# Feed-forward layers of a hybrid encoder by seven block products of sums instead of eight plain ones

## The chip, the cores and the metric

The kernel runs on one core of one Trainium2 chip. The metric is the device time of one execution in microseconds (us); less is better. The engines are TensorE (PE, with its weight loads as PEld), VectorE (DVE), ScalarE (ACT), GpSimd (POOL) and SyncE (SP), which issues nearly all DMA. Each engine works through its own queue in order and waits on semaphores.

## The reference, cut to what matters

1536 tokens of 1024 features (a sequence of 1024 and one of 512) pass one encoder layer in float32. The middle part (a long convolution and a retention mixer) is not touched by the change.

```python
def swiglu(h, w1, w3, w2):
    return (jax.nn.silu(h @ w1) * (h @ w3)) @ w2      # w1, w3 [1024, 2816], w2 [2816, 1024]
...
    h = rmsnorm(x, p['ffn1_pre_g'])
    x = x + 0.5 * rmsnorm(swiglu(h, p['ffn1_w1'], p['ffn1_w3'], p['ffn1_w2']), p['ffn1_post_g'])
    h = rmsnorm(x, p['mix_pre_g'])
    ...                                               # w_in, the two mixers, w_out
    x = x + rmsnorm(y, p['mix_post_g'])
    h = rmsnorm(x, p['ffn2_pre_g'])
    x = x + 0.5 * rmsnorm(swiglu(h, p['ffn2_w1'], p['ffn2_w3'], p['ffn2_w2']), p['ffn2_post_g'])
```

## The kernel before, in words

Activations lie as features (128 partitions, eight blocks) by tokens. Every float32 operand of a matmul is split into a float32r head (`hi_act`, a copy on ACT) and the rest (`lo`, a subtraction on DVE or POOL), and every product is three matmuls (`mm3`, lines 66 to 68): head by head, head by rest, rest by head.

A feed-forward layer (`ffn_phase`) takes the tokens in three groups of 512. `ffn_up` loops over 22 blocks of 128 hidden features; each block loads 1 MB of weights (w1 and w3 together), splits them, and makes 2 times 8 times 3 matmuls of 512 columns into two banks of PSUM. The factor of the first rmsnorm is applied behind the matmuls (L205, L207), so the matmuls do not wait for it. `proj` then makes 22 times 8 times 3 matmuls with w2, and `post` normalizes, adds the residual and stores, 512 tokens at a time. In source order the next group's `norm_T` stands ahead of `proj`, and the last part of `post` runs while the next group's up matmuls run. The splits of weights go to DVE and POOL in turn. The first layer's last group is followed by the norm for `w_in`; the second layer's first norm stands behind the last `out_proj`, with its pools opened early.

A tile scheduler with a timeline of its own sets the order in which each engine's instructions stand, within what data and buffers allow; a pool's `bufs` is the number of buffers that its tiles share.

Of the kernel before, what the change touches and what calls it, by code (L numbers as in the profile page):

```python
# [15 lines left out]
D = 1024  # L16
# [30 lines left out]
class Kern:  # L47
# [16 lines left out]
    def mm3(self, ps, ah, al, bh, bl, first, last):  # L64
        mm = self.nc.tensor.matmul
        mm(ps, lhsT=ah, rhs=bh, start=first, stop=False)  # L66
        mm(ps, lhsT=ah, rhs=bl, start=False, stop=False)  # L67
        mm(ps, lhsT=al, rhs=bh, start=False, stop=last)  # L68
# [16 lines left out]
    def rstd(self, ssq, scale, half=False, eng=None):  # L85
        """(ssq * scale + eps) ** -0.5, times a half when asked"""
# [15 lines left out]
    def rstd_rows(self, acc, psp, rp, tag, half=False, **kw):  # L102
        """acc [128, 512]: sums of squares left to add over the partitions -> DRAM row: the factor of
        rmsnorm of each of the 512 columns; and the tile that can take it"""
# [8 lines left out]
        out = rp.tile([128, 512], F32, tag=tag, name="rrow", **(kw or {"bufs": 1}))  # L113
# [3 lines left out]
        r = self.rstd(c, 1.0 / D, half)  # L117
        row = self.dp.tile([1, 512], F32, name=f"row{self.rows}")
        self.rows += 1
        nc.sync.dma_start(row.rearrange("o (p c) -> (o p) c", c=4), r)  # L120
        return row, out
# [12 lines left out]

    def add_sq(self, acc, x, out, first):
# [9 lines left out]
    def norm_T(self, src, gi, psp, hp, late, row, eng=None, between=None, xp=None):  # L145
# [7 lines left out]
        if row is not None:  # L153
            r = self.np.tile([128, 512], F32, tag="rpre", name="rrow", bufs=1)
            nc.sync.dma_start(r, row.broadcast_to([128, 512]))
        else:
            acc = self.np.tile([128, 512], F32, tag="acc", name="acc", bufs=1)
        for i in range(4):
            x = self.xp.tile([128, 2, 512], F32, tag="x", name="x") if xp is None else \
                xp.tile([128, 2, 512], F32, tag=f"z{2 * i}", name="x", bufs=1)  # L160
            nc.sync.dma_start(x, src[i])
            if i == 1 and between:
                between()
            for j in range(2):
                k = 2 * i + j
                g = self.gains[:, gi, k:k + 1]
                if late:
                    nc.scalar.activation(hh[:, k], x[:, j], AF.Copy, scale=g)  # L168
                    nc.vector.scalar_tensor_tensor(hl[:, k], x[:, j], g, hh[:, k].bitcast(F32), ALU.mult, ALU.subtract)  # L169
                else:  # L170
                    nc.vector.scalar_tensor_tensor(x[:, j], x[:, j], g, r, ALU.mult, ALU.mult)
                    self.hi_act(hh[:, k], x[:, j])
                    self.lo(eng or nc.vector, hl[:, k], x[:, j], hh[:, k])
            if row is None:
                self.add_sq(acc, x, x, i == 0)
        if row is None:
            row, r = self.rstd_rows(acc, psp, self.np, "rpre")
            nc.sync.dma_start(r, row.broadcast_to([128, 512]))
        return (hh, hl, r) if late else (hh, hl)

    def ffn_up(self, hT, w13, up, psp, wp, rp, first=None):
        nc = self.nc
        hh, hl, r = hT
        th, tl = [], []
        for f in range(NF):
            u = up[f * len(up) // NF]
            th.append(u.tile([128, 512], F32R, tag=f"th{f}", name="th"))
            tl.append(u.tile([128, 512], F32R, tag=f"tl{f}", name="tl"))
            raw = None if f else first
            if raw is None:  # L190
                raw = rp.tile([128, 2, KD, 128], F32, tag="raw", name="raw")
                nc.sync.dma_start(raw, w13[f])
            pab = []
            for i in range(2):
                wh = wp.tile([128, KD, 128], F32R, tag="w", name="wh")
                wl = wp.tile([128, KD, 128], F32R, tag="w", name="wl")
                self.hi_act(wh, raw[:, i])
                self.lo(nc.vector if i or first is raw else nc.gpsimd, wl, raw[:, i], wh)
                ps = psp.tile([128, 512], F32, tag="mm", name="up")
                for k in range(KD):  # L200
                    self.mm3(ps, wh[:, k], wl[:, k], hh[:, k], hl[:, k], k == 0, k == KD - 1)
                pab.append(ps)
            hid = self.tp.tile([128, 512], F32, tag="hid", name="hid", bufs=2)
            b = self.tp.tile([128, 512], F32, tag="b", name="b", bufs=1)
            nc.vector.tensor_tensor(hid, pab[0], r, ALU.mult)  # L205
            nc.scalar.activation(hid, hid, AF.Silu)
            nc.vector.tensor_tensor(b, pab[1], r, ALU.mult)  # L207
            nc.gpsimd.tensor_tensor(hid, hid, b, ALU.mult)  # L208
            self.hi_act(th[f], hid)
            self.lo(nc.vector, tl[f], hid, th[f])  # L210
        return th, tl
# [23 lines left out]
    def post(self, src, dst, gi, half, zp, psp, rows=None, op=None, cols=False):  # L235
# [6 lines left out]
        whole = op and op.tile([128, KD, 512], F32R, tag="hh", name="o").bitcast(F32)  # L242

        def done(m, ps):
# [9 lines left out]
            if op and m < 4:  # L254
                nc.sync.dma_start(whole[:, 2 * m:2 * m + 2], src[m])
            if m < KD - 1:
                return
            if cols:
                r = self.rstd_cols(acc, psp, half)
            else:  # L260
                row, r = self.rstd_rows(acc, psp, zp, "rpost", half)
                nc.sync.dma_start(r, row.broadcast_to([128, 512]))
            if rows is not None:
                a2 = zp.tile([128, 512], F32, tag="acc2", name="acc2", bufs=1)
            for i in range(4):
                if op:
                    o = whole[:, 2 * i:2 * i + 2]
                else:
                    o = self.xp.tile([128, 2, 512], F32, tag="x", name="o")
                    nc.sync.dma_start(o, src[i])  # L270
                for j in range(2):
                    nc.vector.tensor_tensor(z[i][:, j], z[i][:, j], r, ALU.mult)  # L272
                    (nc.gpsimd if j else nc.vector).tensor_tensor(z[i][:, j], z[i][:, j], o[:, j], ALU.add)  # L273
                    if op:
                        nc.sync.dma_start(dst[i][:, j], z[i][:, j])
                if not op:
                    nc.sync.dma_start(dst[i], z[i])
                if rows is not None:
                    self.add_sq(a2, z[i], o, i == 0)
            if rows is not None:  # L280
                rows.append(self.rstd_rows(a2, psp, self.xp, "x", bufs=2)[0])
        return done
# [706 lines left out]
```

## Time and profile before

| | |
|---|---|
| median of 3 runs | 3430.8 us (3430.15 to 3433.55) |
| span of the profiled execution | 3430.4 us |
| PE busy, matmuls | 3268.4 us, 95%, 15094 |
| DVE, POOL, ACT busy | 1925.7, 1290.4, 1175.4 us |
| DMA | 422.89 MB, mean 123 GB/s |

The profiled execution has no time of its own beside its span; the span is 0.4 us under the median. Matmuls are pipelined: one of 512 columns is shown as 390 ns long, but the next starts about 226 ns after it. So PE's work is to be counted by starts, not by durations. The layers of the change take 0 to 1102 us and about 2290 to 3411 us of the span.

### The profile page before, as it was taken

To read this page: it belongs to the slowest core of one execution; us is meant where nothing else is said; L and a number is where in the kernel's file an instruction comes from. 1 tells how busy PE (TensorE), PEld (TensorE's weight loads), DVE (VectorE), ACT (ScalarE), POOL (GpSimd) and SP (SyncE) were. 2 spreads that over 40 slices of the span, in tenths; PEclk is the share of its full clock that TensorE was granted. 3 is DMA by queue.
4 is the path that set the end of the run, shared out by engine and by line. 5 is a ranking of instruction groups with operands and counts; after the bars stand their busy time and mean duration, and the time that the engine had idled before them with its cause. 6 is when DMAs were issued, how large, how long until landed. Compare 5 with 4: busy or idle time off the path is not lost. (4 is left out here: it accounts for less than half of the span.)

```text
span 3430.4 us, 39206 instructions
## 1 busy us (share of the span) xinstructions
PE 3268.4 (95%) x15094; PEld 2710.5 (79%) x15094; DVE 1925.7 (56%) x2408; ACT 1175.4 (34%) x1603; POOL 1290.4 (38%) x788
## 2 busy tenths in 40 slices
PE   9999999999999899988989997989999999999998
PEld 7888788887887677766778887868888888888886
DVE  5443544435442599888877879886442444334432
ACT  4333333323332234344544344343232232323221
POOL 3332333234322422368743535554332333233322
PEclk9999999999999999989999999999999999999999
DMA  4223332324232534444354125464223432334232
GB/s 151 98 98 114 138 111 98 114 102 147 99 117 86 196 110 154 155 161 117 97 164 165 44 93 183 129 226 159 98 98 108 149 107 98 114 102 147 94 115 74
DMA packets 123275, 422.89 MB, mean 123 GB/s; under 512 B 28496, under 2 KB 37840, under 8 KB 95696
## 3 DMA queue, kind: packets, MB, share of 16 engines
q1 hardware_dynamic: 123088, 420.38, 36.1%
q8 instruction: 119, 1.95, 0.2%
q14 instruction: 68, 0.56, 0.1%
HBM read 355.73 MB, written 64.54 MB: 123 GB/s over the span
## 5 line engine op out<-in xcount | busy, mean ns | idle before, releaser
L66 PE MATMUL up<-hh,wh 128*128 128x512 f32 x2112 | 824.3, 390 | 8.3 <-ACT hh L168 8.3
L67 PE MATMUL up<-hl,wh 128*128 128x512 f32 x2112 | 824.6, 390 | 0.1
L68 PE MATMUL up<-hh,wl 128*128 128x512 f32 x2112 | 824.4, 390 | 0.0
L59 ACT ACTIVATE wh<-raw 128x1024 fp32r<-128x1024 f32 x312 | 330.0, 1058 | 783.5 <-PE up L67 635.3
L62 POOL TENSOR_TENSOR wl<-raw,wh 128x1024 fp32r<-128x1024 f32 x167 | 411.0, 2461 | 336.6 <-ACT wh L59 302.4
L208 POOL TENSOR_TENSOR hid<-hid,b 128x512 f32<-128x512 f32 x132 | 173.7, 1316 | 856.4 <-DVE b L207 830.6
L66 PEld LDWEIGHTS up<-hh,wh 128*128 128x128 f32 x2112 | 398.4, 189 | 91.3 <-ACT hh L168 8.3
L67 PEld LDWEIGHTS up<-hl,wh 128*128 128x128 f32 x2112 | 398.0, 188 | 83.4 <-DVE hl L169 0.6
L68 PEld LDWEIGHTS up<-hh,wl 128*128 128x128 f32 x2112 | 398.1, 188 | 83.0 <-DVE wl L62 0.4
L62 POOL TENSOR_TENSOR w2l<-raw,w2h 128x1024 fp32r<-128x1024 f32 x98 | 240.6, 2456 | 490.9 <-ACT w2h L59 490.9
L68 PE MATMUL proj<-th,w2l 128*128 128x512 f32 x1056 | 410.8, 389 | 0.0
L66 PE MATMUL proj<-th,w2h 128*128 128x512 f32 x1056 | 410.8, 389 | 0.0
L67 PE MATMUL proj<-tl,w2h 128*128 128x512 f32 x1056 | 410.8, 389 | 0.0
L62 DVE TENSOR_TENSOR tl<-hid,th 128x512 fp32r<-128x512 f32 x132 | 262.8, 1991 | 234.2 <-ACT th L59 233.9
L59 ACT ACTIVATE w2h<-raw 128x1024 fp32r<-128x1024 f32 x172 | 181.8, 1058 | 472.8 <-PE proj L67 364.0
L207 DVE TENSOR_TENSOR b<-up,rrow 128x512 f32<-128x512 f32 x132 | 91.1, 690 | 373.8 <-PE up L68 372.9
L62 DVE TENSOR_TENSOR w2l<-raw,w2h 128x1024 fp32r<-128x1024 f32 x74 | 101.3, 1369 | 326.6 <-ACT w2h L59 326.4
L66 PE MATMUL wips<-hh,wh 128*128 128x512 f32 x576 | 231.2, 401 | 22.0 <-DVE o L464 8.6
L66 PEld LDWEIGHTS proj<-th,w2h 128*128 128x128 f32 x1056 | 198.2, 188 | 41.2
L67 PEld LDWEIGHTS proj<-tl,w2h 128*128 128x128 f32 x1056 | 198.2, 188 | 41.2
L68 PEld LDWEIGHTS proj<-th,w2l 128*128 128x128 f32 x1056 | 198.2, 188 | 41.1
L67 PE MATMUL wips<-hl,wh 128*128 128x512 f32 x576 | 230.3, 400 | 0.0
(250 smaller groups left out, 5296.4 us busy)
## 6 DMA issues: line engine op xcount, KB each, us to landing
raw<-ffn_w SPq DMA_DIRECT2D x197, 1024.0 KB, 4.8
raw<-w_in_f SPq DMA_DIRECT2D x48, 512.0 KB, 3.7
x<-x SPq DMA_DIRECT2D x36, 512.0 KB, 4.5
o<-x SPq DMA_DIRECT2D x36, 512.0 KB, 5.0
x<-z SPq DMA_DIRECT2D x24, 512.0 KB, 4.2
raw<-w_out SPq DMA_DIRECT2D x24, 512.0 KB, 4.6
raw<-w_in_v SPq DMA_DIRECT2D x16, 512.0 KB, 3.8
tap<-fold SPq DMA_DIRECT2D x8, 1024.0 KB, 4.9
```

What stands on the lines that cost most here:

```text
L59: self.nc.scalar.activation(hi, src, AF.Copy)
L62: eng.tensor_tensor(lo, src, hi.bitcast(F32), ALU.subtract)
L66: mm(ps, lhsT=ah, rhs=bh, start=first, stop=False)
L67: mm(ps, lhsT=ah, rhs=bl, start=False, stop=False)
L68: mm(ps, lhsT=al, rhs=bh, start=False, stop=last)
L207: nc.vector.tensor_tensor(b, pab[1], r, ALU.mult)
L208: nc.gpsimd.tensor_tensor(hid, hid, b, ALU.mult)
```

## The change

Both feed-forward layers are rewritten (`ffn`). The tokens form two groups of 768, each in two halves of 384. A product of a weight matrix cut in 2 by 2 blocks with an activation matrix cut in 2 by 2 blocks, which takes eight block products, is made from seven products of sums and differences of blocks. Up (`up_unit`, 22 units for each group): rows of blocks are w1 and w3, the other cut is in the 1024 features. Seven products of 4 times 3 matmuls of 384 columns go into three banks; DVE makes four sums of weight blocks, all seven rests, and the combinations of products. Down (`down`): the cuts are in the 2816 hidden features, the 1024 outputs and the tokens. Five of the seven weight operands are sums; they are made once for each layer by `weight_sums`, which runs beside group 0's units (two steps for each unit), and kept in DRAM (`ws`). The rmsnorm is now applied to the activations ahead of the matmuls (`normed`, `operands`); group 1's normalized tokens go through DRAM (`nx`). Sums and differences of activations are made by DVE from whole quads [128, 4, 384]. In these layers POOL keeps only the power in `rstd`. x1 and x2 lie in quads, and the mixer and `out_proj` read and write 512-token groups in pieces of them (`pieces`).

```diff
+    def normed(self, src, gi, pool, row):
+        xs = []
+        for kh in range(2):
+            x = self.quad(pool, "xq")
+            nc.sync.dma_start(x, src[kh])
+            xs.append(x)
+        if row is None:
+            r = self.spread(self.rstd3(self.sum_sq(xs, pool)))
+        else:
+            r = self.half("rq")
+            nc.sync.dma_start(r, row.broadcast_to([128, 384]))
+        for kh in range(2):
+            for k in range(4):
+                g = self.gains[:, gi, 4 * kh + k:4 * kh + k + 1]
+                nc.vector.scalar_tensor_tensor(xs[kh][:, k], xs[kh][:, k], g, r, ALU.mult, ALU.mult)
+        return xs
...
+        product(ba, a11, "11", True)
+        nc.scalar.activation(p1, ba, AF.Copy)
+        tt(s[0], a21, a22, ALU.add)
+        tt(s[1], s[0], a11, ALU.subtract)
+        product(bb, s[1], "t2", True)
+        tt(u2, bb, p1, ALU.add)
+        product(ba, a12, "21", False)
+        nc.scalar.activation(hid[0], ba, AF.Silu)
+        tt(s[2], a11, a21, ALU.subtract)
+        product(bb, s[2], "t3", False)
+        tt(u3, bb, p1, ALU.add)
+        product(bc, s[0], "t1", True)
+        tt(u3, bc, u3, ALU.add)
+        product(bb, a22, "t4", False)
+        tt(p1, bb, p1, ALU.add)
+        tt(hid[0], hid[0], p1, ALU.mult)
+        tt(s[3], a12, s[1], ALU.subtract)
+        product(bc, s[3], "22", False)
+        tt(u2, bc, u2, ALU.add)
+        nc.scalar.activation(u2, u2, AF.Silu)
+        tt(hid[1], u2, u3, ALU.mult)
...
+    def weight_sums(self, w2, pool):
+        for p, ((a, *more), _) in self.FORMS.items():
+            for c in range(4) if more else ():
+                n = min(3, 11 - 3 * c)
+                ts = []
+                for q in (a, more[0]):
+                    t = self.quad(pool, "wsum").rearrange("p a b -> p (a b)")[:, :512 * n].rearrange("p (f c) -> p f c", c=512)
+                    nc.sync.dma_start(t, w2[q[0], q[1], 3 * c:3 * c + n].rearrange("f p c -> p f c"))
+                    ts.append(t)
+                nc.vector.tensor_tensor(ts[0], ts[0], ts[1], ALU.add if more[1] > 0 else ALU.subtract)
+                nc.sync.dma_start(self.ws[p][c][:, :n], ts[0])
+                yield
...
+    def post_quads(self, z, src, dst, gi, Y, row, g):
+        for th in range(2):
+            r = self.spread(self.rstd3(self.sum_sq([z[0, th], z[1, th]], Y), True))
+            for mh in range(2):
+                t = z[mh, th]
+                o = self.quad(Y, "res")
+                nc.sync.dma_start(o, src[mh][th])
+                for k in range(4):
+                    nc.vector.scalar_tensor_tensor(t[:, k], t[:, k], self.gains[:, gi, 4 * mh + k:4 * mh + k + 1], r, ALU.mult, ALU.mult)
+                for k in range(0, 4, 2):
+                    nc.vector.tensor_tensor(t[:, k:k + 2], t[:, k:k + 2], o[:, k:k + 2], ALU.add)
+                    nc.sync.dma_start(dst[mh][th][:, k:k + 2], t[:, k:k + 2])
+            if row is not None:
+                r = self.rstd3(self.sum_sq([z[0, th], z[1, th]], Y))
+                c = 768 * g + 384 * th
+                nc.sync.dma_start(row[:, c:c + 384].rearrange("o (c p) -> (o p) c", p=128), r)
...
+        with pool("xq", 6) as X, pool("yq", 20) as Y, pool("fr", 5) as self.fr, pool("fs") as self.fs, \
+                pool("fw", 10) as self.fw, pool("ft", 6) as self.ft, pool("pm", 8, space=PSUM) as self.pm:
...
+            for g in range(2):
+                for f in range(NF):
+                    self.up_unit(w13[f], [hid[fh, th][c][:, i] for th in range(2)])
+                    if f:
+                        for _ in range(2):
+                            next(side, None)
...
+                z = self.down(w2, hid, Y, at)
+                self.post_quads(z, srcs[g], dsts[g], post, Y, row_out, g)
```

How the scheduler now orders the engines is seen at three places. First PE before, in layer 1 where the first group's down products (`proj`) end and the next group's up products begin:

```order
1586 L67 MATMUL proj<-tl,w2h 128x512
1587 L68 MATMUL proj<-th,w2l 128x512
1588 L66 MATMUL up<-hh,wh 128x512
1589 L67 MATMUL up<-hl,wh 128x512
...
1622 L67 MATMUL up<-hl,wh 128x512
1623 L111 MATMUL ss<-sqs,onesr 128x512
1624 L68 MATMUL up<-hh,wl 128x512
```

The norm's sums (`ss`) stand 35 matmuls deep among the next group's up products. PE now at the end of layer 1's first group (`dn` the down products, `ss` the sums over partitions, `rps` the spread factors, `ua` the next group's first up product):

```order
2689 L69 MATMUL dn<-xh,w2l 128x384
2690 L205 MATMUL ss<-ones,acc 128x1 x3
2691 L212 MATMUL rps<-ident,r 128x128 x3
2692 L205 MATMUL ss<-ones,acc 128x1 x6
2693 L212 MATMUL rps<-ident,r 128x128 x3
2694 L205 MATMUL ss<-ones,acc 128x1 x3
2695 L67 MATMUL ua<-b11h,wh 128x384
```

All sums and spreads of both halves moved between the last down product and the first up product. DVE now at the same place (`z` the four quads of outputs, `sq` and `acc` the sums of squares, `res` the residual), from the last combination of products to the first half's last addition:

```order
653 L349 TENSOR_TENSOR z<-z,dn 128x384 x6
654 L298 TENSOR_TENSOR s_5782<-raw 128x512
655 L62 TENSOR_TENSOR wl<-s_5636,wh 128x512
656 L192 TENSOR_TENSOR sq<-sq 128x768
...
660 L195 TENSOR_TENSOR acc<-sq,acc 128x384
661 L94 TENSOR_SCALAR m<-ss 128x3
...
666 L406 SCALAR_TENSOR_TENSOR z<-z,gains,rps 128x384 x8
667 L408 TENSOR_TENSOR z<-z,res 128x768 x4
```

Behind them stand the second half's same steps and the sums for the stored factor, and only then the next group's rests of weights. The last place is SP in layer 1's first units (`raw` 256 KB of up weights, `wsum` loads of second weights, `ws` stores of their sums):

```order
6 L272 DMA raw<-ffn_w 128x512 x9
7 L329 DMA wsum<-ffn_w 128x3x512 x6
8 L329 DMA wsum<-ffn_w 128x2x512 x2
9 L272 DMA raw<-ffn_w 128x512
10 L329 DMA wsum<-ffn_w 128x3x512 x2
11 L272 DMA raw<-ffn_w 128x512
12 L332 DMA ws_1_0_179<-wsum 128x1536
13 L329 DMA wsum<-ffn_w 128x3x512
...
20 L272 DMA raw<-ffn_w 128x512 x4
21 L332 DMA ws_2_1_184<-wsum 128x1536
22 L272 DMA raw<-ffn_w 128x512 x9
```

The loads of second weights stand in bursts of eight, ahead of single loads of up weights.

## Rows read from the trace of the kernel before

**Rows 1.** The page's first part: busy us, share and instructions by engine.
```profile
PE 3268.4 (95%) x15094; PEld 2710.5 (79%) x15094; DVE 1925.7 (56%) x2408; ACT 1175.4 (34%) x1603; POOL 1290.4 (38%) x788
```
**Rows 2.** Windows: start:end, length, busy us (and instructions) by engine, granted clock, DMA share, GB/s.
```profile
0.00:100.00 100.00, 91.59 (x392) 75.33 (x393) 49.19 (x54) 41.20 (x51) 30.92 (x23) 1.00 0.44 151
200.00:420.00 220.00, 220.00 (x972) 182.15 (x971) 96.40 (x104) 69.38 (x83) 67.55 (x34) 1.00 0.34 115
2450.00:2700.00 250.00, 250.00 (x1105) 207.00 (x1104) 88.39 (x84) 72.81 (x87) 70.24 (x35) 1.00 0.31 105
```
**Rows 3.** Groups by line and shape: engine, tiles, shape, count | busy us, mean ns.
```profile
L67 PE MATMUL up<-hl,wh 128*128 128x512 f32 x2112 | 824.6, 390 | 0.1
L67 PE MATMUL proj<-tl,w2h 128*128 128x512 f32 x1056 | 410.8, 389 | 0.0
```
**Rows 4.** Timeline, PE and PEld in the transforms: start us, length us (first and last of runs).
```profile
1900.16 0.28 PE L66 MATMUL fw<-th,mh 128*128 128x256 f32 x1
...
1903.95 0.28 PE L68 MATMUL fw<-th,ml 128*128 128x256 f32 x1
...
1906.87 0.19 PEld L68 LDWEIGHTS fw<-th,ml 128*128 128x128 f32 x1
1906.99 0.19 PEld L66 LDWEIGHTS fw<-th,mh 128*128 128x128 f32 x1
```
**Rows 5.** Windows around a wait of PE in the retention stage.
```profile
1702.00:1707.00 5.00, 5.00 (x23) 4.06 (x22) 4.96 (x10) 1.69 (x2) 1.49 (x2) 1.00 0.28 78
1710.30:1713.30 3.00, 2.96 (x7) 2.38 (x8) 2.71 (x6) 1.70 (x4) 1.77 (x5) 0.50 0.35 124
```
**Rows 6.** Timeline of the end: start us, length us, engine, line, tiles.
```profile
3410.65 0.39 PE L68 MATMUL proj<-th,w2l 128*128 128x512 f32 x1
3413.25 1.55 PE L128 MATMUL ssc<-ones,pacc 128*128 128x1 f32 x8 [2.21 <-DVE pacc L251]
3415.08 1.02 POOL L94 TENSOR_TENSOR r<-m,mhalf 128x4 f32<-128x4 f32 x1 [22.46 <-DVE m L93]
3416.13 0.16 DVE L95 TENSOR_TENSOR c<-r 128x4 f32<-128x4 f32 x1 [1.13 <-POOL r L94]
3417.03 1.09 PE L132 MATMUL rps<-ident,r 128*128 128x128 f32 x4 [2.23 <-DVE r L99]
3418.16 4.87 DVE L272 TENSOR_TENSOR z<-z,rps 128x512 f32<-128x512 f32 x8 [1.27 <-PE rps L132]
3422.95 3.71 DVE L273 TENSOR_TENSOR z<-z,o 128x512 f32<-128x512 f32 x4
```
**Rows 7.** Timeline of the start.
```profile
6.17 1.06 ACT L59 ACTIVATE wh<-raw 128x1024 fp32r<-128x1024 f32 x1 [3.85 <-DMA raw<-ffn_w]
8.40 2.73 DVE L169 SCALAR_TENSOR_TENSOR hl<-x,gains,hh 128x512 fp32r<-128x512 f32 x4
```
**Rows 8.** Instructions of line 59 and line 62: count: ns min/median/max, first and last start.
```profile
L59 ACT ACTIVATE w2h<-raw x172: 1039/1061/1065, 240.2 to 3394.5; 128x1024 fp32r<-128x1024 f32 x172
L59 ACT ACTIVATE sqs<-acc x9: 630/632/635, 22.0 to 2388.4; 128x512 fp32r<-128x512 f32 x9
L62 DVE TENSOR_TENSOR wl<-raw,wh x145: 1206/1225/2589, 7.3 to 3276.0; 128x1024 fp32r<-128x1024 f32 x145
L62 DVE TENSOR_TENSOR tl<-tr,th x96: 673/679/693, 1818.7 to 2204.3; 128x512 fp32r<-128x512 f32 x96
```
**Rows 9.** Windows in which DMA is full.
```profile
5.00:10.00 5.00, 1.59 (x3) 0.99 (x4) 2.74 (x4) 3.52 (x5) 0.00 (x0) 1.00 1.01 404
1150.00:1155.00 5.00, 5.00 (x23) 4.10 (x22) 3.16 (x4) 0.00 (x0) 1.43 (x2) 0.95 1.02 364
1800.00:1805.00 5.00, 4.19 (x19) 3.19 (x18) 1.89 (x2) 1.70 (x2) 2.64 (x6) 1.00 1.02 337
```
**Rows 10.** Windows behind layer 1, and behind the last `out_proj` weights.
```profile
1100.00:1110.00 10.00, 6.34 (x25) 4.36 (x24) 3.07 (x3) 3.59 (x5) 4.48 (x2) 0.98 0.40 19
1110.00:1120.00 10.00, 10.00 (x39) 8.07 (x38) 4.85 (x5) 3.48 (x5) 5.68 (x5) 0.85 0.78 305
1120.00:1130.00 10.00, 6.78 (x30) 5.18 (x28) 7.37 (x8) 2.67 (x4) 8.57 (x6) 1.00 0.45 152
1130.00:1140.00 10.00, 7.87 (x26) 5.48 (x24) 4.65 (x6) 1.65 (x3) 6.81 (x5) 0.83 0.36 80
1140.00:1150.00 10.00, 2.88 (x7) 2.33 (x8) 9.86 (x10) 2.95 (x3) 5.07 (x3) 0.68 0.40 152
2270.00:2290.00 20.00, 12.53 (x35) 8.46 (x34) 18.34 (x20) 11.30 (x17) 11.78 (x5) 0.76 0.67 223
```
**Rows 11.** DMA issues: tiles, queue, count, KB each, median us to landing.
```profile
x<-x SPq DMA_DIRECT2D x36, 512.0 KB, 4.5
rrow<-row SPq DMA_DIRECT2D x14, 256.0 KB, 3.5
nc<-rrow SPq DMA_DIRECT2D x14, 2.0 KB, 4.3
```

More of the change, by code (lines that the diff above doesn't have):

```diff
@@ L62, in lo, with mm3 @@
         eng.tensor_tensor(lo, src, hi.bitcast(F32), ALU.subtract)
[L64 to L68, printed above, removed]
+    def mm3(self, ps, ah, al, bh, bl, first, last, more=False):
+        mm, kw = self.nc.tensor.matmul, {"skip_group_check": True} if more else {}
+        mm(ps, lhsT=ah, rhs=bh, start=first, stop=False, **kw)
+        mm(ps, lhsT=ah, rhs=bl, start=False, stop=False, **kw)
+        mm(ps, lhsT=al, rhs=bh, start=False, stop=last, **kw)
     def setup(self):
@@ L100, in rstd, with rstd_rows @@
         return r
-    def rstd_rows(self, acc, psp, rp, tag, half=False, **kw):
+    def rstd_rows(self, acc, psp, rp, tag, row, **kw):
         nc = self.nc
@@ L116, in rstd_rows @@
         nc.sync.dma_start(c, out[0:1].rearrange("o (p c) -> o p c", c=4))
-        r = self.rstd(c, 1.0 / D, half)
-        row = self.dp.tile([1, 512], F32, name=f"row{self.rows}")
-        self.rows += 1
+        r = self.rstd(c, 1.0 / D)
         nc.sync.dma_start(row.rearrange("o (p c) -> (o p) c", c=4), r)
-        return row, out
     def rstd_cols(self, acc, psp, half):
@@ L133, in rstd_cols, with pieces @@
         return ps
+    def pieces(self, t, quads, g, i):
+        kh, k = divmod(2 * i, 4)
+        a, end = 512 * g, 512 * g + 512
+        while a < end:
+            q, o = divmod(a, 384)
+            n = min(384 - o, end - a)
+            s = a - 512 * g
+            yield t[:, :, s:s + n], quads[q // 2][kh][q % 2][:, k:k + 2, o:o + n]
+            a += n
     def add_sq(self, acc, x, out, first):
@@ L152, in norm_T @@
         hl = hp.tile([128, KD, 512], F32R, tag="hl", name="hl")
[L153 to L157, printed above, removed]
-        for i in range(4):
[L159 to L163, printed above, removed]
+        r = self.np.tile([128, 512], F32, tag="rpre", name="rrow", bufs=1)
@@ new lines, in sum_sq @@
+    def sum_sq(self, xs, pool):
+        nc = self.nc
+        acc = self.half("acc")
+        for i, x in enumerate(xs):
+            sq = self.quad(pool, "sq")
+            nc.scalar.activation(sq, x, AF.Square)
+            nc.vector.tensor_tensor(sq[:, 0:2], sq[:, 0:2], sq[:, 2:4], ALU.add)
+            if i:
+                nc.vector.tensor_tensor(acc, sq[:, 0], acc, ALU.add)
+                nc.vector.tensor_tensor(acc, sq[:, 1], acc, ALU.add)
+            else:
+                nc.vector.tensor_tensor(acc, sq[:, 0], sq[:, 1], ALU.add)
+        return acc
@@ new lines, in rstd3, with spread @@
+    def rstd3(self, acc, half=False):
+        nc = self.nc
+        ss = self.bank("ss")[:, :3]
+        for t in range(3):
+            nc.tensor.matmul(ss[:, t:t + 1], lhsT=acc[:, t * 128:(t + 1) * 128], rhs=self.one, start=True, stop=True)
+        return self.rstd(ss, 1.0 / D, half)
+    def spread(self, r):
+        ps = self.bank("rps")
+        for t in range(3):
+            self.nc.tensor.transpose(ps[:, t * 128:(t + 1) * 128], r[:, t:t + 1].broadcast_to([128, 128]), self.ident)
+        return ps
@@ new lines, in down, with ev @@
+    def down(self, w2, hid, Y, at):
+        nc = self.nc
+        tt = nc.vector.tensor_tensor
+        z, banks = {}, {}
+        def ev(q, ps, first, sign=1):
+            if first:
+                z[q] = self.quad(Y, "z")
+            for m in range(4):
+                if first:
+                    nc.scalar.activation(z[q][:, m], ps[m], AF.Copy)
+                else:
+                    tt(z[q][:, m], z[q][:, m], ps[m], ALU.add if sign > 0 else ALU.subtract)
+        for p, old in ((1, None), (4, None), (7, 1), (3, None), (5, None), (6, 3), (2, None)):
+            (a, *am), (b, *bm) = self.FORMS[p]
+            ps = banks[p] = banks[old] if old else [self.bank("dn") for _ in range(4)]
+            for c in range(3):
+                n = 4 if c < 2 else 3
+                xh, xl = self.quad(Y, "xh", F32R), self.quad(Y, "xl", F32R)
+                if not bm:
+                    self.hi_act(xh[:, :n], hid[b][c][:, :n])
+                    self.lo(nc.vector, xl[:, :n], hid[b][c][:, :n], xh[:, :n])
+                for i in range(n):
+                    f = 4 * c + i
+                    if bm:
+                        t = self.half("bs")
+                        tt(t, hid[b][c][:, i], hid[bm[0]][c][:, i], ALU.add if bm[1] > 0 else ALU.subtract)
+                        self.hi_act(xh[:, i], t)
+                        self.lo(nc.vector, xl[:, i], t, xh[:, i])
+                    raw = self.fr.tile([128, 512], F32, tag="raw", name="raw2")
+                    nc.sync.dma_start(raw, self.ws[p][f // 3][:, f % 3] if am else w2[a[0], a[1], f])
+                    wh = self.fw.tile([128, 4, 128], F32R, tag="w", name="w2h")
+                    wl = self.fw.tile([128, 4, 128], F32R, tag="w", name="w2l")
+                    raw = raw.rearrange("p (m c) -> p m c", c=128)
+                    self.hi_act(wh, raw)
+                    self.lo(nc.vector, wl, raw, wh)
+                    for m in range(4):
+                        self.mm3(ps[m], wh[:, m], wl[:, m], xh[:, i], xl[:, i], f == 0 and not old, f == 10, old is not None)
+            if p == 1:
+                ev((1, 1), ps, True)
+            elif p == 4:
+                ev((0, 0), ps, True)
+                ev((1, 0), ps, True)
+            elif p == 7:
+                ev((0, 0), ps, False)
+            elif p == 3:
+                ev((0, 1), ps, True)
+            elif p == 5:
+                ev((0, 0), ps, False, -1)
+                ev((0, 1), ps, False)
+            elif p == 6:
+                ev((1, 1), ps, False)
+            else:
+                ev((1, 0), ps, False)
+                ev((1, 1), ps, False, -1)
+            at(p)
+        return z
@@ L233, in proj, with post @@
                         done(m, ps)
-    def post(self, src, dst, gi, half, zp, psp, rows=None, op=None, cols=False):
+    def post(self, src, dst, g, gi, zp, psp, row):
         nc = self.nc
@@ L253, in done @@
                 nc.vector.tensor_copy(acc, sq)
-            if op and m < 4:
-                nc.sync.dma_start(whole[:, 2 * m:2 * m + 2], src[m])
             if m < KD - 1:
                 return
[L258 to L264, printed above, removed]
-            for i in range(4):
[L266 to L270, printed above, removed]
+            r = self.rstd_cols(acc, psp, False)
+            a2 = zp.tile([128, 512], F32, tag="acc2", name="acc2", bufs=1)
+            for i in range(4):
+                o = self.xp.tile([128, 2, 512], F32, tag="x", name="o")
+                for part, q in self.pieces(o, src, g, i):
+                    nc.sync.dma_start(part, q)
                 for j in range(2):
```

225 lines of the change are left out of this document (129 added, 96 removed), and 3 rows, old and new, of the table FORMS.

## Prediction

> **What bounds the kernel now.** The page's first part comes first: PE is busy for 3268.4 of 3430.4 us, DVE for 56% [rows 1]. Then windows inside the feed-forward layers, since a mean hides stages: in 200 to 420 and in 2450 to 2700 us PE never waits, at a granted clock of 1.00, that is 2.4 GHz, with DVE below half [rows 2]. The stages to be changed are bound by PE alone; its waits lie elsewhere, at the start, behind layer 1 and ahead of layer 2 [rows 2, 10]. PE's work must be counted by starts: 1105 matmuls in 250 us are 0.2262 us each, while one is shown as 390 ns long [rows 2, 3].
>
> The groups by line [rows 3] give the count before: up is 3 times 2112, `proj` 3 times 1056, together 9504, or 2149.8 us.
>
> **What it removes.** Now 22 blocks of 7 products of 12 matmuls, in 2 groups and 2 layers, make 7392 for up; `down` is half of that, 3696. That is 11088 matmuls of 384 columns. No row shows such a matmul. One of 256 columns stands in the transforms: 33 starts between 1900.16 and 1903.95, 0.1184 us each [rows 4]. I take 384 as midway, (0.2262 + 0.1184) / 2 = 0.1723, so 1910.5 us and a **gain of 239**. The bounds: 0.1697, in proportion to the 512-column row (28 more gain), and 0.188 if the weight loads, 0.19 long, stood one behind the other (a loss of 174 against my value). I exclude most of the upper end because loads of 0.19 already follow 0.12 apart in those rows.
>
> The Trainium skill (Trainium Kernel Development and Optimization, Best Practices) wants the distance to the bound judged by the busy share of weight loads, not of matmuls. That share is 79% here [rows 1]; the count of loads grows by a sixth, and by that reading alone there would be no gain of 239 but the loss of the upper end. The rows above, in which loads overlap, speak against it.
>
> **Does DVE keep the pace?** A unit of up lasts 84 × 0.1723 = 14.5 us. DVE does 7 rests and 4 weight sums of 512 columns, 0.609 apart (4.87 for eight) [rows 6], and 7 combinations of 384. The slope between 512 and 1024 columns is (1225 − 679) / 512 = 1.07 ns a column [rows 8], so a 384 costs 0.47, a 768 0.88 and a 1536 1.70. Together 10.0 of 14.5 us. It fits; DVE's queue also stands behind combinations that wait for a product, for which 4.5 us are spare. ACT's copies and evictions (0.63 for 512 columns [rows 8]) fit as well. The sums of second weights add 15 × 1.70 + 5 × 1.14 = 31 us of DVE to each layer, some 3 in each of about ten units: 13 of 14.5. So I cost DVE at nothing inside the units, but this is the closest fit of all.
>
> **What it adds**, with T the end of the last matmul at each place. These are costs because PE's order has nothing to do there: where `ss` stood 35 matmuls deep among up products, it now stands ahead of them.
>
> A, start of layer 1: the first product needs normalized and combined quads. First data at about 6 us (the first copy starts at 6.17 [rows 7]), a square 1.49 (ACT, 1536 columns by its own slope, [rows 8]); then DVE's first 50 instructions, added up at these prices and 0.55 for a scaled copy of 384 (2.73 / 4 for 512 [rows 7]): weight rests and sums 9.8, quads 11 × 1.70, 16 scalings 8.8, adds of squares 6.3, small ones 2.4, 46 in all, with 2 of waits 55. Five products (10.3) run earlier, so 45 are lost. Before, 392 matmuls stand in the first 100 us [rows 2], so 11 were lost. **+34.**
>
> B, transfers of the sums: each layer reads 110 slices of 0.262 MB and writes half, 43 MB, beside 42 of the up loads (11 MB), in about 10.5 units (152 us). Full DMA moved 404, 364 and 337 GB/s [rows 9]; at 370, 54 MB are 147 us, and some 26 us pass before the bursts begin, in which only raw loads run: 173 against 152. SP issues in order with the raw loads behind bursts of eight. **+20 for each layer**, bounds 0 and 40: **+40.**
>
> The Trainium skill (DMA: Bandwidth & Descriptors, Bandwidth) gives 425 GB/s for a 16 MB read by one core. By that, 54 MB take 128 us, an estimate, and B would be near nothing. The windows here stay at 337 to 404, with full queues, so the sum goes by them.
>
> C, norm of group 1 in layer 1: two `ss` and two spreads stand in PE's queue with nothing between. Two chains of add and `ss`, POOL's power (1.02), small steps and the spread (1.1) [rows 6] with the squares ahead are 23. After such a wait PE's clock is granted at half: 7 matmuls in 3 us at 0.50 (1.2 GHz) against 23 in 5 [rows 5], about 1.6 us. **+25.**
>
> D, end of group 0 in layer 1: PE waits for the whole `post`. Evictions to T + 3.0, squares 4.1, adds 7.3, `ss` to spread 11.3, scalings 15.7, additions 19.2, the second half's sums (its own row sums among them) 25.6, spread 30.8, scalings and additions 38.7, row sums 42.2, `ss` 43.0. With the cold clock **+45.**
>
> E, end of layer 1: the same to T + 43, then `rstd`, the row's store, its loads back in broadcast (3.5 to 4.5 each [rows 11]), x loads behind them in SP, the norm and the weights for `w_in`: PE is full again at T + 62 to 64, having lost some 57. Before, 1100 to 1150 held 127 matmuls [rows 10], 28.7 of 50 us, so 21 were lost. **+36.**
>
> F, start of layer 2: its loads stand in SP behind the stores of x2 (landing at T + 21.5), then DVE has 34.6 of norm and quads: T + 56, less 10.3 of early products, 45. Before, 2270 to 2290 held 35 matmuls [rows 10], 12 lost; I credit 5, as part of that stays. **+40.**
>
> G, end of group 0 in layer 2, which stores no row: T + 22.4, cold clock: **+24.**
>
> H, the tail: the same 22.4 and then scalings 4.4, additions 3.5, the last write 3.7: 34.0, against 19.4 from 3411.0, the end of the last matmul, to the span's end [rows 6]. **+15.**
>
> I, small waits, estimated from the rest: banks of PSUM in `down` (an eviction of 384 costs 0.5), 8.5 of DVE for group 1's norm in layer 2, and the turn from up to `down`: **+14.**
>
> Sum of losses 34 + 40 + 25 + 45 + 36 + 40 + 24 + 15 + 14 = 273; net +34. The profiled execution's 3430.4 becomes 3464; the median of the runs is 0.4 higher, so **3465 us**, 1.0% slower. Runs of this kernel can tell about 0.2%, 7 us, from no change.
>
> **The rivals.** First, the other side: SP's queue is no limit. If loads are served beside the stores and weight sums, B's two terms of 20 fall away, and the loads of E and F land 4.5 us earlier (one x load [rows 11]): 3465 − 49 = 3416, faster. For it: a burst at 404 [rows 9], and `down` needs the sums only after the last unit. Against it: every rest that DVE does in a unit needs that unit's raw load, which stands behind a burst. It decides when DMA is below full in the first ten units; some 41 of 273 must go for the time to be faster than 3424.
>
> Second, DVE sets the pace of up: combinations that wait for PE block the next unit's rests in its queue, and one us is added to each of 88 units: 3465 + 88 = 3553. For it: 13 of 14.5 us in ten units; against it: 10 of 14.5 in all others.
>
> Third, the change does not do what it says for PE: weight loads bind, 0.188 a start, 3465 + 174 = 3639. Against it [rows 4].
>
> Fourth, the two sides cancel: 3431. For it: nine estimated terms of 15 to 45 whose errors may sum to 34.
>
> **How the numbers follow.** Forecast 0.58, with a range of its own of 3424 to 3510, of which 0.03 lies within 0.2% of before; transfers hidden 0.22; DVE's pace 0.12; weight loads 0.03; cancelling 0.05. Faster by over 0.2%: 0.22. Within 0.2%: 0.05 + 0.03 = 0.08. Slower: 0.55 + 0.12 + 0.03 = 0.70. The range reaches down to 3400, below the first rival's 3416, since a start of 0.1697 would take 28 more off, and up to 3535, short of the second rival's 3553 and the third: some 0.2 left out.
>
> **What would show it.** Right: in the steady units PE without waits and 0.172 us from start to start; 11088 matmuls; one stretch of PE idle at each of A, C, D, E, F, G and H with DVE busy in it, longest at E and F; DMA near 1.0 in the first ten units of each layer, with PE waiting for `raw` there. Wrong: starts nearer 0.19; idle time of PE ended by DVE in every unit; PE going on through the group ends, or waits there of half these lengths; DMA well below full with no wait for `raw`.

## The result, and the profile after

| | before | changed |
|---|---|---|
| median of 4 runs | 3431.5 us | 3472.6 us (3469.1 to 3475.1) |
| ratio, 95% interval | 1 | 1.0117 (1.0101 to 1.0133) |
| profiled execution: its span | 3430.4 us | 3466.4 us |
| PE matmuls | 15094 | 16776 |

The change made the kernel 1.2% slower. The page's first part, which answers to [rows 1], shows less PE time and more DVE time in a longer span:

```profile
PE 3078.7 (89%) x16776; PEld 2882.6 (83%) x16776; DVE 2688.7 (78%) x4340; ACT 1425.3 (41%) x2357; POOL 611.3 (18%) x439
```

Whether a matmul of 384 columns costs what was forecast is seen in the starts on PE's timeline, in one of layer 1's first units:

```profile
85.77 0.33 PE L68 MATMUL ua<-b11l,wh 128*128 128x384 f32 x1
...
90.11 0.34 PE L69 MATMUL uc<-b22h,wl 128*128 128x384 f32 x1
93.48 0.44 PE L67 MATMUL ub<-t2h,wh 128*128 128x384 f32 x1 [3.03 <-ACT wh L59]
```

25 steps in 4.34 us are 0.1736 each; over long stretches it is 0.1733 to 0.1734, and the latter is used below. By the same count a 512 of before takes 0.2267 (the windows of [rows 2] hold one or two matmuls too many at their edges). So the matmuls give 9504 × 0.2267 - 11088 × 0.1734 = 232 us. Where they went is seen in windows of the places that the prediction calls A, B (two of them), C, a steady unit, D, E, F, G and H (columns as in [rows 2]):

```profile
0.00:50.00 50.00, 15.39 (x55) 13.47 (x55) 38.82 (x58) 20.99 (x21) 2.62 (x8) 1.00 0.32 117
90.00:100.00 10.00, 6.97 (x29) 6.15 (x28) 9.66 (x15) 4.12 (x8) 0.00 (x0) 0.83 1.02 414
170.00:180.00 10.00, 5.96 (x19) 5.94 (x20) 9.77 (x13) 3.34 (x6) 0.00 (x0) 0.67 0.89 312
230.00:280.00 50.00, 21.29 (x102) 20.39 (x103) 30.80 (x58) 12.05 (x15) 1.70 (x2) 0.66 0.48 173
300.00:320.00 20.00, 20.00 (x118) 20.00 (x117) 14.95 (x27) 7.53 (x14) 0.00 (x0) 1.00 0.25 67
580.00:640.00 60.00, 25.44 (x120) 24.39 (x121) 41.50 (x81) 15.73 (x17) 3.70 (x4) 0.63 0.32 107
1110.00:1170.00 60.00, 7.56 (x30) 6.42 (x30) 33.61 (x68) 11.38 (x10) 3.75 (x5) 0.52 0.60 150
2380.00:2430.00 50.00, 14.87 (x39) 11.43 (x40) 41.90 (x56) 19.63 (x21) 4.89 (x4) 0.54 0.49 168
2940.00:2950.00 10.00, 2.38 (x9) 2.39 (x10) 8.16 (x17) 0.00 (x0) 4.10 (x1) 0.50 0.39 157
3440.00:3460.00 20.00, 4.09 (x18) 3.52 (x18) 16.29 (x35) 0.00 (x0) 5.25 (x2) 0.50 0.20 79
```

In the steady unit PE runs without a wait at the full clock; at the other places it stands for 30 to 87% of the window, with DVE busy for most of it, and the granted clock is below 1.00 at all of them but the first. DMA is near full only at B. The waits in total (what, how often, longest) name the links:

```profile
PE ss L205 <- DVE acc L195: 121.1, 14, 13.4
PE rps L212 <- DVE r L100: 41.7, 12, 8.4
PE ub L67 <- ACT wh L59: 23.7, 5, 5.8
```

The end of group 0 in layer 1 (D) shows them in PE's timeline, from the last down product:

```profile
578.19 0.34 PE L69 MATMUL dn<-xh,w2l 128*128 128x384 f32 x1
585.68 1.44 PE L205 MATMUL ss<-ones,acc 128*128 128x1 f32 x6 [7.15 <-DVE acc L195]
589.10 0.90 PE L212 MATMUL rps<-ident,r 128*128 128x128 f32 x3 [1.97 <-DVE r L100]
602.30 1.44 PE L205 MATMUL ss<-ones,acc 128*128 128x1 f32 x6 [12.30 <-DVE acc L195]
604.82 1.44 PE L205 MATMUL ss<-ones,acc 128*128 128x1 f32 x6 [1.08 <-DVE acc L195]
608.23 0.90 PE L212 MATMUL rps<-ident,r 128*128 128x128 f32 x3 [1.97 <-DVE r L100]
620.68 1.44 PE L205 MATMUL ss<-ones,acc 128*128 128x1 f32 x6 [11.55 <-DVE acc L195]
621.99 0.67 PE L67 MATMUL ua<-b11h,wh 128*128 128x384 f32 x1
622.45 0.52 PE L68 MATMUL ua<-b11l,wh 128*128 128x384 f32 x1
```

T is 578.4: spread at T + 10.7 to 11.6, the second at T + 30.7, up again at T + 43.6, first at half clock (0.32 a start). The forecast had 11.3, 30.8 and 43.0.

The table gives the time lost at each place: the length of the stretch between two PE starts, less the feed-forward matmuls that start in it times 0.1734 (before: 0.2267). "Through unit 5" is until 420 up matmuls are issued. D and G begin with group 0's last down product; the other products of that `down` are in the rest of the layer. The columns behind the second are kernels of the next section.

| place | before | changed | b_no_traffic | c_norm_unit | dg_post_unit | all_covered | two_kept |
|---|---|---|---|---|---|---|---|
| A, start through unit 5 | 11.6 | 49.8 | 44.4 | 48.2 | 49.6 | 52.3 | 49.8 |
| B and C, rest of group 0's up | | 46.0 | 30.0 | 21.8 | 45.8 | 17.6 | 6.0 |
| D, through unit 5 of group 1 | | 46.1 | 45.6 | 45.7 | 8.5 | 8.5 | 9.6 |
| rest of layer 1 | 14.8 (B to here) | 4.4 | 4.4 | 4.2 | 13.4 | 13.7 | 13.4 |
| E, to the first w_in product | 43.5 | 106.2 | 106.7 | 105.3 | 108.0 | 108.0 | 92.8 |
| mixer, to the last out_proj | 1183.3 | 1155.3 | 1160.2 | 1168.7 | 1165.4 | 1162.1 | 1157.2 |
| F, through unit 5 of layer 2 | 2.1 | 60.3 | 54.8 | 60.9 | 60.4 | 67.7 | 62.2 |
| B of layer 2 | | 12.9 | 2.1 | 13.4 | 12.7 | 8.1 | 6.6 |
| G, through unit 5 of group 1 | | 24.8 | 24.8 | 24.6 | 13.5 | 10.9 | 11.1 |
| rest of layer 2 | 1.1 (B to here) | 4.4 | 4.4 | 4.3 | 5.4 | 5.3 | 6.4 |
| H, tail | 19.5 | 33.1 | 33.1 | 33.1 | 33.1 | 33.1 | 25.0 |
| sum | 1275.9 | 1543.3 | 1510.5 | 1530.2 | 1515.8 | 1487.3 | 1440.1 |

The mixer row, which none of the edits below touches, lies between 1155 and 1169 from one execution to the next. So a place is compared in this table, and a sum by the timed runs.

### The profile page after: what moved, and what is told of

Same layout as the page of the kernel before. It is cut to its first block, busy times and chain, and to the rows that moved or that the text cites. A ratio compares the mean times of both kernels' runs of the same rounds, so it can differ in the third digit from the quotient of the medians.

```text
span 3466.4 us, 46334 instructions
## 1 busy us (share of the span) xinstructions
PE 3078.7 (89%) x16776; PEld 2882.6 (83%) x16776; DVE 2688.7 (78%) x4340; ACT 1425.3 (41%) x2357; POOL 611.3 (18%) x439
## 5 line engine op out<-in xcount | busy, mean ns | idle before, releaser
L68 PE MATMUL dn<-xl,w2h 128*128 128x384 f32 x1232 | 411.3, 334 | 3.3 <-DVE xl L62 3.3
L62 DVE TENSOR_TENSOR wl<-s,wh 128x512 fp32r<-128x512 f32 x352 | 241.9, 689 | 207.3 <-ACT wh L59 104.5
L67 PE MATMUL dn<-xh,w2h 128*128 128x384 f32 x1232 | 389.5, 335 | 1.6 <-ACT xh L59 1.6
L69 PE MATMUL dn<-xh,w2l 128*128 128x384 f32 x1232 | 388.5, 334 | 0.0
L59 ACT ACTIVATE w2h<-raw 128x512 fp32r<-128x512 f32 (+1 forms) x348 | 237.0, 682 | 330.5 <-PE dn L68 222.5
L68 PEld LDWEIGHTS dn<-xl,w2h 128*128 128x128 f32 x1232 | 231.2, 188 | 4.6 <-DVE xl L62 4.6
L67 PEld LDWEIGHTS dn<-xh,w2h 128*128 128x128 f32 x1232 | 228.8, 188 | 3.4 <-ACT xh L59 2.9
L69 PEld LDWEIGHTS dn<-xh,w2l 128*128 128x128 f32 x1232 | 229.2, 188 | 0.0
L69 PE MATMUL wips<-hh,wl 128*128 128x512 f32 x576 | 228.2, 396 | 0.0
L62 DVE TENSOR_TENSOR wl<-raw,wh 128x512 fp32r<-128x512 f32 (+1 forms) x276 | 198.1, 718 | 20.3 <-ACT wh L59 17.7
L62 POOL TENSOR_TENSOR wl<-raw,wh 128x1024 fp32r<-128x1024 f32 x36 | 93.4, 2595 | 221.0 <-ACT wh L59 171.2
## 6 DMA issues: line engine op xcount, KB each, us to landing
ws<-wsum SPq DMA_DIRECT2D x30, 768.0 KB, 11.1
```

The source lines that it names most:

```text
L59: self.nc.scalar.activation(hi, src, AF.Copy)
L62: eng.tensor_tensor(lo, src, hi.bitcast(F32), ALU.subtract)
L67: mm(ps, lhsT=ah, rhs=bh, start=first, stop=False, **kw)
L68: mm(ps, lhsT=ah, rhs=bl, start=False, stop=False, **kw)
L69: mm(ps, lhsT=al, rhs=bh, start=False, stop=last, **kw)
```

## The experiments

Times below are medians; the kernel before stood at 3429.4 to 3430.5 us beside them. "Changed" is 3472.6, 1.0117 times the time of before.

**Steps for the norm and for the post.** Theory: PE loses time at C, D and G because a chain between engines has nothing between its links in PE's queue. The rival throughout: DVE has no time to spare.

```diff
-                    xs = ready(1, th)
...
+                    acc = self.sum_sq(xs, Y)
+                    yield
+                    r = self.rstd3(acc)
+                    yield
+                    r = self.spread(r)
+                    yield
```

> Group 1's norm in the first of the two feed-forward layers is given out in steps (squares and their sums, ss, spread, scaling), one or two for each unit, in place of in one piece; nothing else changes. Theory (PE loses about 33 us at that place because ss and rps stand in its queue with nothing between them): the two waits of PE between about 234 and 268 us go, 28 to 33 us less than the change's 3472.6, so 3440 to 3445. Rival (DVE is what lacks time there, so its 16 us for the norm delay the units all the same): 3455 or more.

Measured 3461.6 (1.0088, 1.0066 to 1.0111): B and C fell from 46.0 to 28.8. Without transfers C alone is 30.0, which puts 16.0 on B; if B stayed as it was, 12.8 of C are left.

```diff
-            r = self.spread(self.rstd3(self.sum_sq([z[0, th], z[1, th]], Y), True))
+            acc = self.sum_sq([z[0, th], z[1, th]], Y)
+            yield
+            r = self.rstd3(acc, True)
+            yield
+            r = self.spread(r)
+            yield
...
-                    if f:
+                    if f or g:
```

> The post of group 0 in both layers runs in steps beside the first units of group 1; the posts at the ends of the layers stay as they are. Theory (the 44 and 24 us lost at the two group ends are chains of DVE, PE, POOL that nothing covers, and a unit has 4.5 us of DVE to spare): PE goes on with up products, 60 to 68 us less, 3405 to 3413. Rival (DVE has no time beside the units: 38 and 19 us of its work go into four units, so it is late by what does not fit into 4 x 4.5): about 25 us come back, 3430.

Measured 3457.1 (1.0078, 1.0061 to 1.0094): D fell from 46.1 to 28.6, G from 24.8 to 20.3. Both runs fell short of the theory: the first came out where its rival put it, the second short of its rival too. But PE's waits for `ss` were still there (12.7 us in the first, 6.8 in the second), since the driver took two steps for a unit, which put squares and `ss` side by side again. With one step for each unit:

```diff
-                    if f:
-                        for _ in range(2):
-                            next(side, None)
+                    for _ in range(2 if f else 0):
+                        next(sums, None)
+                    for _ in range(f > 10):
+                        next(side, None)
```

> Group 1's norm in layer 1 again in steps, but one step (squares and sums; ss and the power; spread, scaling and store) for each unit, so that a whole unit of 84 products stands between two steps; in c_norm_steps two steps fell into one unit, and ss still waited 12.7 us for its sums. Theory (what is lost is distance between producer and consumer in PE's queue, not DVE's time): PE waits for no ss there, the first group's up loses 13 to 17 us in place of 46, 3438 to 3445. Rival (DVE's time): no better than c_norm_steps, 3455 to 3465.

Measured 3448.5 (1.0056, 1.0033 to 1.0078): 24 us less. Of the 21.8 that are left of B and C, 8 stand behind a wait in the units with transfers (PE stands from 167 to 172), and 10 where PE waits 6.5 us for the copy `p` at 244, behind squares that wait for their loads. Of that wait more below. For group 0's post:

```diff
+                    for _ in range(1 if g else 2 if f else 0):
+                        next(side, None)
```

> Group 0's post in steps, one for each of group 1's units, in place of two for each unit, which left 28.6 of 46 us lost in layer 1 and 20 of 25 in layer 2. Theory (distance): PE waits for no ss or spread there, 5 to 8 us are left at each of the two ends, 55 to 60 us less than the change's 3472.6, 3412 to 3418. Rival (DVE lacks time in those units, as the waits for wl and p in dg_post_steps suggest): no better than dg_post_steps, about 3450 to 3457.

Measured 3437.5 (1.0025, 1.0014 to 1.0036): 35 less than changed, not 55 to 60. D is 8.5 and G 13.5, but the rest of layer 1 rose by 9. Most of that lies at 669, where the second half's squares hold the copy `p` in ACT's queue, PE waits 3.7 us for it, and the granted clock is 0.70 to 0.74 until 677. With the same instructions as in the run with two steps the kernel is 19.6 us faster, and no wait of PE for `ss` is left in these units. At C distance, that is how much of PE's own work stands between the links of a chain, is the cause of the wait for `ss` and DVE's time is not: in c_norm_steps DVE was busy for only 8.75 of the 15 us around it (235 to 250), while the chain began with a load that ACT waited 4.1 us for. At D and G the two theories are not fully apart, since one step for each unit also gives DVE's work twice as many units: in dg_post_steps DVE was busy without a pause from 614 to 630, and PE waited 1.9 us for its `wl` there. Distance is shown for the waits for `ss`; how much of the other gain is DVE's time is not.

**The transfers of the sums (B).**

```diff
-                nc.vector.tensor_tensor(ts[0], ts[0], ts[1], ALU.add if more[1] > 0 else ALU.subtract)
+                nc.vector.tensor_tensor(ts[0][:, :1, :8], ts[0][:, :1, :8], ts[1][:, n - 1:n, :8], ALU.add)
```

> The sums of second weights are loaded and stored as in the change, but the additions of 1536 and 1024 columns on DVE are cut to 8 columns each (the stored blocks are then not sums, so the output is another). Theory (the waits in the first ten units come from the transfers: raw loads of 256 KB behind bursts of wsum loads with DMA full): the time stays within 6 us of the change's 3472.6. Rival (the 31 us of DVE additions in each layer make the waits): 25 to 30 us less, about 3445.

Measured 3470.7 (1.0122, 1.0106 to 1.0139): unchanged, so DVE's additions cost nothing that shows in the time. The loads and stores were still made, and waited for, in this run.

```diff
-                yield from self.weight_sums(w2, Y)
+                for _ in range(20):
+                    yield
...
-self.ws[p][f // 3][:, f % 3] if am else w2[a[0], a[1], f]
+w2[a[0], a[1], f]
```

> No sums of second weights are made: no wsum loads, no stores, no additions; down reads the first block of each form directly (the output is another). Theory (transfers): the 29 us that PE loses in the first ten units of the two layers go, 3440 to 3447. Rival (the losses there come from the units themselves, their in-order waits between PE, ACT and DVE): within 6 us of 3472.6.

Measured 3440.8 (1.0030, 1.0018 to 1.0042): 31.8 less, all of it at A, B and F (37.7 by the table, in which the mixer moved the other way). The two runs together put B on the transfers and what waits for them. How they reach PE is shown only in part. SP's timeline of the changed kernel, around the wait of PE at 168 to 174, has three loads of up weights behind two stores that wait for their sums:

```profile
161.09 1.04 SPq L329 DMA_DIRECT2D wsum<-ffn_w  x2
164.63 7.67 SPq L332 DMA_DIRECT2D ws<-wsum  x2
172.57 3.10 SPq L272 DMA_DIRECT2D raw<-ffn_w  x3
```

But these loads are not what this wait of PE ends with. PE waits for the head of a sum of up weights (`s`), which DVE makes from 171.85 on without having waited for a load: it stands in DVE's queue behind the last combination of the unit before and an addition of second weights.

```profile
169.71 0.56 DVE L311 TENSOR_TENSOR hid<-u,u 128x384 f32<-128x384 f32 x1
170.18 1.75 DVE L331 TENSOR_TENSOR wsum<-wsum 128x1536 f32<-128x1536 f32 x1
171.85 0.69 DVE L291 TENSOR_TENSOR s<-raw 128x512 f32<-128x512 f32 x1
```

With additions of 8 columns PE's wait here falls from 5.5 to 3.8 us, and another of 2.0 comes at 109; without transfers both are gone. SP's order shows at C: the loads of the norm go out at 236.0, behind a store that waited for its sum until 235.6, and PE's first wait for `ss` is 12.9 us, where it is 6.8 without transfers. So of the 16.0 that B and C lose by the transfers in layer 1, 8.6 lie in the units behind the wait at 168 and 7.5 at C.

**All of it, with fewer sums in a unit.**

```diff
+                    for _ in range((1 + f % 2) if f else 0):
+                        next(sums, None)
+                    for _ in range(1 if g or f else 0):
+                        next(side, None)
```

> Both of these together, group 1's norm moved to units 1 to 6, and the sums of second weights given out at three steps for two units in place of four, so that DMA moves about 4.6 MB in a unit, some 315 GB/s, in place of 5.8 MB and 395. Theory: C, D and G go as in the two runs before, and of the 29 us lost to transfers under 8 are left: 110 to 120 us less than the change's 3472.6, 3350 to 3365, and faster than the kernel before. Rival (DVE, now with 10 us of its own, 2.3 of sums and up to 8 of a step in a 14.6 us unit, becomes the limit): the units take 1 to 3 us longer while steps run, 3385 to 3410.

Measured 3411.3 (0.9949, 0.9931 to 0.9968): faster than before, but some 50 short of the theory and just above the 3385 to 3410 of its rival. The places named did fall (table), while A, F and the rest of layer 1 rose by 19 together. ACT's and PE's timelines show the largest new wait:

```profile
139.58 1.48 ACT L191 ACTIVATE sq<-xq 128x1536 f32<-128x1536 f32 x1 [7.41 <-DMA xq<-x]
141.43 1.48 ACT L191 ACTIVATE sq<-xq 128x1536 f32<-128x1536 f32 x1 [0.37 <-DMA xq<-x]
142.82 0.47 ACT L290 ACTIVATE p<-ua 128x384 f32<-128x384 f32 x1
```
```profile
143.34 0.69 PE L67 MATMUL ua<-b21h,wh 128*128 128x384 f32 x1 [11.75 <-ACT p L290]
```

A square that waits for its load holds the copy `p` behind it in ACT's queue, and PE may add to the bank only when `p` has been copied from it. So three edits on top of this kernel:

```diff
                         nc.sync.dma_start(xs[kh], srcs[1][kh][th])
+                    yield
```

> all_covered with one step more: the loads for group 1's norm go out one unit ahead of the squares that need them. In all_covered PE waited 12.1 us at 143.3 for the copy p, which stood in ACT's queue behind squares that wait for their loads. Theory (the wait of PE is that of the squares, passed on by ACT's order): that wait falls to under 3 us, and something of the same at the start of layer 2, in all 9 to 13 us less than all_covered's 3411.3, 3398 to 3402. Rival (DMA is full there whatever the order, so that the loads come as late): within 3 us of 3411.

Measured 3395.3 (0.9897, 0.9882 to 0.9912): 16 less; B and C fall from 17.6 to 6.0. The wait was the square's.

```diff
-        b["t1"] = self.split(Y, t1, "t1")
+        b["t1"] = self.split(Y, t1, "t1", self.nc.gpsimd)
...
```

> all_covered with three of the seven rests of activation quads (t1, t4, b22; 1536 columns each) on POOL, which has next to nothing to do in these layers. Theory (the starts of both layers, A and F, are bound by DVE's 46 and 35 us): three times 1.7 us come off DVE at either start and are not missed elsewhere, 6 to 10 us less, 3401 to 3406. Rival (the starts hang on loads, squares and the chain of ss, not on DVE's sum; or POOL's rest of a quad, some 3.8 us by 2.595 for 1024 columns, comes too late for product t1): within 3 us of 3411, or more.

Measured 3434.1 (1.0014, 1.0003 to 1.0026): 23 more, a miss. DVE's and POOL's timelines at the start:

```profile
46.06 5.99 POOL L62 TENSOR_TENSOR t1l<-t,t1h 128x1536 fp32r<-128x1536 f32 x1 [15.73 <-ACT t1h L59]
52.01 3.92 POOL L62 TENSOR_TENSOR t4l<-t,t4h 128x1536 fp32r<-128x1536 f32 x1
55.89 3.87 POOL L62 TENSOR_TENSOR b22l<-xq,b22h 128x1536 fp32r<-128x1536 f32 x1
```
```profile
49.09 3.51 DVE L62 TENSOR_TENSOR wl<-s,wh 128x512 fp32r<-128x512 f32 x1
52.63 3.85 DVE L307 TENSOR_TENSOR s<-raw,s 128x512 f32<-128x512 f32 x1
56.40 3.90 DVE L62 TENSOR_TENSOR wl<-raw,wh 128x512 fp32r<-128x512 f32 x1
60.69 0.68 DVE L62 TENSOR_TENSOR wl<-s,wh 128x512 fp32r<-128x512 f32 x1
```

Three DVE instructions of 512 columns take 3.5 to 3.9 us while POOL subtracts, and 0.68 again when it is done: the two engines took turns, and A rose from 52.3 to 59.6. So this run says nothing on whether DVE's sum bounds A.

```diff
-((1, None), (4, None), (7, 1), (3, None), (5, None), (6, 3), (2, None))
+((1, None), (4, None), (7, 1), (3, None), (5, None), (2, None), (6, None))
...
+                    if p == 6 and f in (0, 5, 8):
+                        tick()
```

> all_covered with the seven products of down in another order, so that the first half of tokens is complete one product (22.9 us) before the end, and at the end of both layers its ss, spread and scaling run beside that last product. Theory (E and H are the post's chain behind the last matmul, as priced: T + 3, 4.1, 7.3, 11.3 and so on): the tail falls from 33 to about 22 us and the end of layer 1 to the first w_in product from 108 to about 88, 3411 less 28 to 34, 3377 to 3383. Rival for E (what lasts there is the row's store, its broadcast and the loads in SP's queue behind it, not the post): the tail's 11 alone, 3400.

Measured 3389.6 (0.9882, 0.9867 to 0.9897): 21.7 less; the tail falls from 33.1 to 25.0, E from 108.0 to 94.6. Both theories had a size wrong: the post is on the path at E as at H, and each gains 8 to 13 us, not 11 and 20.

> The three edits of load_ahead, rests_on_pool and half_first together. Theory: they lie at different places, so that their gains add, 45 to 57 us less than all_covered, 3355 to 3368. Rival (a gain at one place is given back at the next, as in the first runs of this study): 3380 or more.

Measured 3395.6 (0.9901, 0.9885 to 0.9916): short by the rests on POOL, as the last run shows.

> load_ahead and half_first together, with all rests of activations back on DVE. Theory (the two gains lie at different places and add; what kept all_three from it were the rests on POOL alone): 3411.3 less 16.0 and less 21.7, 3370 to 3378, a ratio to the kernel before of about 0.983 to 0.985. Rival (one gain takes from the other, as the 0.3 us between load_ahead and all_three could also be read): 3385 to 3390.

Measured 3375.6 (0.9842, 0.9828 to 0.9855): the two gains add. This is the fastest kernel of the study, 1.6% under the kernel before. PE's share in the page:

```profile
PE 3063.2 (91%) x16776; PEld 2865.1 (85%) x16776; DVE 2691.3 (80%) x4356; ACT 1422.6 (42%) x2357; POOL 606.0 (18%) x439
```

## Why the prediction was right, step by step

The forecast was 3465 us, measured 3472.6 (3466.4 in the profile). By the prediction's own terms, from the table:

- The matmuls: 232 in place of 239. A start of 384 columns is 0.1734, against 0.1723 taken as midway. PE runs the steady units without a wait, so neither the weight loads (third rival: 0.188) nor DVE's pace (second rival) bind.
- A: 49.8 - 11.6 = 38, of which 5.4 go with the transfers: 33 (34 forecast). For A as DVE's sum speaks that from 35 to 60 DVE is busy for 24.96 of the 25 us in the changed kernel, and PE for 17.37; no run took work off DVE there without slowing it, so it is argued and not shown.
- B: 5.4 + 16.0 in layer 1 and 5.5 + 10.8 in layer 2, from the column without transfers, 38 (40 forecast; 31.8 by the timed runs). The size came out, the picture only in part. A full window holds 414 GB/s, above the 370 taken, and DMA was not full throughout: its share is 0.64 to 0.99 in stretches of 30 us between 60 and 210. The waits of PE there were ended by sums of weights on DVE, not by `raw`, and 7.5 of the 21 in layer 1 lie at C's place.
- C: 30 (25). The second half's squares begin only when the scaled first half is stored, which the forecast let overlap: their loads go out at 244.6 and 247.2, 6.5 us from issue to landing by the page, but ACT waits 12.5 us, and the store `nx` ends that wait (row below). Why it hangs on that store, presumably by a buffer that it frees, was not tested.
- D and G: 46 and 25 (45 and 24).
- E, the mixer and F together: 106.2 + 1155.3 + 60.3 against 43.5 + 1183.3 + 2.1, that is +93, 87 without F's transfers (36 + 40 forecast). E alone is up by 63 and F by 58, and the mixer is down by 28 (14 to 28 over the changed kernels), which the forecast took as fixed. At E the moment came out: PE starts again at 1171.8, 64 us behind the last product (62 to 64 forecast). The credit of 21 for what the kernel before loses there did not: from the first `v` product, the first behind the layer, to the first w_in product pass 41.6 us before and 42.3 now (rows below).
- H: 13.6 (15).
- I: 2.1 + 4.4 + 4.4, less the 15.9 that the kernel before loses in its layers: -5 (14 forecast). The step that failed is the credit: small waits of before were taken as none.

The row behind C, of ACT, and PE's behind E in the changed kernel:

```profile
257.43 1.48 ACT L191 ACTIVATE sq<-xq 128x1536 f32<-128x1536 f32 x1 [12.52 <-DMA nx<-xq]
1171.78 1.22 PE L67 MATMUL v<-w2h,hh 128*128 128x512 f32 x2 [21.76 <-ACT w2h L59]
1214.04 0.77 PE L67 MATMUL wips<-hh,wh 128*128 128x512 f32 x1 [6.48 <-DVE vo L725]
```

And PE's in the kernel before:

```profile
1105.50 0.73 PE L66 MATMUL v<-w2h,hh 128*128 128x512 f32 x2 [1.68 <-ACT w2h L59]
1147.12 0.76 PE L66 MATMUL wips<-hh,wh 128*128 128x512 f32 x1 [7.25 <-DVE vo L495]
```

The sum is 33 + 38 + 30 + 46 + 87 + 25 + 14 - 5 = 268 against 273. The errors (matmuls -7, C +5, E and F +11, I -19, the others within 2) nearly cancel, and within E and F so do a credit that did not come and a mixer that got shorter. So the mechanism was right, that uncovered chains cost more than the matmuls save, and that the time was met to 8 us is in part luck. The first rival, that SP's queue is no limit, would not have made the kernel faster: without any transfers of sums it still took 3440.8, 31.8 less and not 49.

## What to carry to other kernels

Fewer products pay only if what stands around them is covered: here 232 us of PE time were bought with 268 us of losses, most of them in chains that cross engines with nothing in PE's queue between their links. Ask of every such chain how much of PE's work is issued between two links: with one step for each 14.6 us unit PE's waits for `ss` were gone, with two steps they were not. Then ask what each link stands in front of in its engine's queue: squares on ACT held a copy that PE needed, in several of the kernels here. A load that an engine waits for also holds what stands behind it in that engine's queue, and so the next engine.

## What the runs showed of the hardware

In two places DVE and POOL did not run beside one another. In rests_on_pool's rows above, DVE's subtractions of 512 columns grew from 0.68 to 3.5 to 3.9 us while POOL subtracted 1536 columns. In the tail of the changed kernel it is POOL that waits: its power of 128x3, 0.85 us long at 29.54 in the start, takes 4.10 beside DVE's additions, as in the rows of DVE and POOL:

```profile
3449.01 3.55 DVE L408 TENSOR_TENSOR z<-z,res 128x768 f32<-128x768 f32 x4
3449.17 4.10 POOL L95 TENSOR_TENSOR r<-m,mhalf 128x3 f32<-128x3 f32 x1 [6.23 <-DVE m L94]
```

The Trainium skill (SBUF — State Buffer, SBUF: two separate sides) says that a DVE instruction with two operands in SBUF and a POOL instruction that reads SBUF exclude each other on a shared pair of ports, and that the one that starts first has the pair for its whole instruction. The rows agree that the two exclude each other; in the tail POOL stood through four DVE instructions, not one.
